# Rotary embedding on one core: two rows of slab 3's cast, instead of three, ahead of the last row of slab 1

## The chip, the cores and the metric

The kernel runs on one core of a Trainium2 chip. The metric is the device time of one launch in microseconds (us). Three runs of the kernel before took 163.22, 163.46 and 164.78 us; their median is 163.46.

## The reference

The input x has 16 batches of 512 positions of 1024 values in float32. The 1024 values are 16 heads of 64, and each head is two halves of 32. Each position has 32 cosines and 32 sines, the same for all heads and batches.

```python
x = x.reshape(batch, seq, num_heads, head_dim)
x1, x2 = x[..., :half_dim], x[..., half_dim:]
rotated = np.concatenate([
    x1 * cos - x2 * sin,
    x1 * sin + x2 * cos
], axis=-1)
return rotated.astype(np.float32)
```

Input and output are 33.55 MB each.

## The kernel before, in words

**Tiles.** The 8192 rows (batch times position) of 1024 values are cut into four pairs of slabs: 0-1, 2-3, 4-5 and 6-7. In a pair each of the 128 partitions holds 16 consecutive rows, 8 of the even slab and 8 of the odd one. A slab is thus 128 partitions x 8192 float32 (32 KB a partition, 4 MB in all). There are three places for a pair in on-chip memory (`places`); pair 6-7 reuses the place of pair 0-1, so its load must wait until that pair has been stored.

**Work on a slab.** All of it is done in place. `cast` (ScalarE) turns the slab's float32 rows into bfloat16 in the lower half of the same bytes. VectorE (lines 171 and 174) multiplies them by the cosine table into the upper half, then by the signed sine table in the lower half, and adds the latter to the former with the two halves of each head exchanged. `copy_out` (ScalarE) turns the upper half back into float32 over the whole slab. All ScalarE work on slabs goes through the helper `copy`, line 155, which keeps the program's order on that engine. `cast` and `copy_out` take a first and a last element, so that a slab's work can be split by rows of `dim` = 1024 elements.

**Tables.** Cosines and sines of 16 positions each lie in partitions 0, 2 ... 62. Eight matmuls with a matrix of ones and minus ones (`pick`) spread them over all partitions, and the result is kept as two bfloat16 tables, one for even and one for odd slabs.

**Transfers.** All are issued by SyncE (SP) through `issue`, line 66, in the program's order, on one queue. Slabs 0 and 1 are loaded one by one, pairs 2-3 and 4-5 in two halves each, first the even partitions (`EVEN`), then the odd ones (`ODD`). All of these are issued in the first 6 us. Then come, in this order: store 0-1 even and odd, load 6-7 even and odd, store 2-3, store 4-5 even and odd, store 6-7. A load of 6-7 waits for the store of the same partitions to land.

**Order around the change.** The loop over `passes` takes slab 0 in two halves, slab 7 in three pieces and every other slab whole. In the pass of a slab the cast of the next slab is issued first, then VectorE's three instructions, then the copy. In the pass of slab 1, ScalarE casts slab 2, copies all rows of slab 1 but the last (`LAST[1]` is one row), casts the first `PART` elements of slab 3, and copies slab 1's last row. Store 0-1 waits for that last row. The rest of slab 3 is cast in the pass of slab 2, from element `PART` on, and VectorE's work on slab 3 waits for that.

Of the kernel before, what the change touches and what calls it, by code (L numbers as in the profile page):

```python
# [2 lines left out]

# [4 lines left out]


@with_exitstack  # L10
def kernel(
    ctx: ExitStack,
    tc: tile.TileContext,
    x: bass.AP,
    cos: bass.AP,
    sin: bass.AP,
    num_heads: int,
    out: bass.AP,
):
    nc = tc.nc  # L20
    P = nc.NUM_PARTITIONS

    batch, seq, dim = x.shape
    nh = num_heads
    hd = dim // nh
    half = hd // 2
    bf16 = mybir.dt.bfloat16
    f32 = mybir.dt.float32

    nb = 2  # L30
    nslabs = batch // nb
    rpp = nb * seq // P
    W = rpp * dim
    TP = seq // (2 * rpp)
    TS = P // TP // 2
    TW = 2 * rpp * half

    out_flat = out.rearrange("b s h d -> b s (h d)")

    singles = ctx.enter_context(tc.tile_pool(name="singles", bufs=1))  # L40
    pairs = ctx.enter_context(tc.tile_pool(name="pairs", bufs=3))
    psum = ctx.enter_context(tc.tile_pool(
        name="psum", bufs=1, space=bass.MemoryType.PSUM))


    def view(t, offset, *dims):
        return dataclasses.replace(t, offset=t.offset + offset,
                                   ap=[t.ap[0], *[list(d) for d in dims]])

    places = [pairs.tile([P, 2 * W], f32, tag="pair", name="pair") for _ in range(3)]


    def here(s, n=1):
        return view(places[s // 2 % 3], s % 2 * W, (1, n * W))


    def there(t, s, n=1):  # L60
        return bass.AP(tensor=t.tensor, offset=t.offset + s // 2 * 2 * P * W + s % 2 * W,
                       ap=[[2 * W, P], [1, n * W]])


    def issue(out, in_):
        tc.keep_in_program_order(nc.sync.dma_start(out=out, in_=in_))  # L66


    def load(s, n=1, parts=slice(None)):
        issue(here(s, n)[parts], there(x, s, n)[parts])  # L70


    def store(s, n=1, parts=slice(None)):
        issue(there(out_flat, s, n)[parts], here(s, n)[parts])


    EVEN, ODD = slice(0, P, 2), slice(1, P, 2)


    load(0)  # L80


    cos_sb = singles.tile([P, TW], f32, tag="cos_sb")
    sin_sb = singles.tile([P, TW], f32, tag="sin_sb")
    for t, src in ((cos_sb, cos), (sin_sb, sin)):
        nc.vector.memset(t, 0.0)  # L86
        issue(t[:TP * TS:TS], bass.AP(
            tensor=src.tensor, offset=src.offset, ap=[[TW, TP], [1, TW]]))

    load(1)  # L90
    for s in (2, 4):
        for parts in (EVEN, ODD):
            load(s, 2, parts)


    pick = singles.tile([P, 2 * P], bf16, tag="pick")
    nc.gpsimd.memset(pick, 0.0)  # L97
    for g in range(2):
        part = view(pick, g * P, (TP, P // TP), (1, TP))
        nc.gpsimd.affine_select(  # L100
            out=part, in_=part, compare_op=mybir.AluOpType.not_equal,
            fill=1.0 - 2.0 * g, base=0, pattern=[[0, P // TP], [-TS, TP]],
            channel_multiplier=1)

    tab1 = singles.tile([P, 2 * TW], bf16, tag="tab1")
    for i, t in enumerate((cos_sb, sin_sb)):
        nc.vector.tensor_copy(out=view(tab1, i * TW, (1, TW)), in_=t)  # L107

    accs, tabs = [], []
    for h in range(2):  # L110
        acc = psum.tile([P, 2 * rpp * hd], f32, tag=f"acc{h}", name="acc")
        for i in range(2):
            for f in range(2):
                nc.tensor.matmul(  # L114
                    view(acc, i * rpp * hd + f * half, (hd, rpp), (1, half)),
                    view(pick, i * f * P, (1, P)),
                    view(tab1, i * TW + h * rpp * half, (half, rpp), (1, half)),
                    start=True, stop=True)
        accs.append(acc)
        tabs.append(singles.tile([P, 2 * rpp * hd], bf16, tag=f"tab{h}", name="tab"))  # L120
    nc.vector.tensor_copy(out=tabs[0], in_=accs[0])  # L121

    PART = 3 * dim
    LAST = {1: dim, 3: dim // 2}
    passes = []
    for s in range(nslabs):
        r = 0  # L130
        for n in {0: (4, 4), nslabs - 1: (4, 2, 2)}.get(s, (rpp,)):
            passes.append((s, r, n))
            r += n


    def halves(u):
        s, r, n = u
        t = here(s).bitcast(bf16)
        return [view(t, (2 * r + i * n) * dim, (1, n * dim)) for i in range(2)]


    def cast(u, a=0, b=None):
        s, r, n = u
        m = (n * dim if b is None else b) - a
        copy(view(halves(u)[0], a, (1, m)), view(here(s), r * dim + a, (1, m)))


    def copy_out(u, a=0, b=None):
        s, r, n = u
        m = (n * dim if b is None else b) - a  # L150
        copy(view(here(s), r * dim + a, (1, m)), view(halves(u)[1], a, (1, m)))


    def copy(out, in_):
        tc.keep_in_program_order(nc.scalar.copy(out=out, in_=in_))  # L155


    for i, u in enumerate(passes):
        s, r, n = u
        if i == 0:  # L160
            cast(u)
            cast(passes[1])
            copy(tabs[1], accs[1])
            cast(passes[2])
        elif s > 0 and not r:
            for v in passes:
                if v[0] == s + 1:
                    cast(v, PART if v[0] == 3 else 0)
        lo, up = halves(u)
        for t, a in ((up, 0), (lo, rpp * hd)):  # L170
            nc.vector.tensor_mul(  # L171
                out=t, in0=lo,
                in1=view(tabs[s % 2], a + r * hd, (hd, n), (0, nh), (1, hd)))
        nc.vector.tensor_add(  # L174
            out=up, in0=up, in1=view(lo, half, (hd, n * nh), (-half, 2), (1, half)))

        if s == 1:
            copy_out(u, 0, n * dim - LAST[s])
            cast((3, 0, rpp), 0, PART)
            copy_out(u, n * dim - LAST[s])  # L180
            for act in (store, load):
                for parts in (EVEN, ODD):
                    act(0 if act is store else 6, 2, parts)
        elif s == 3:
            copy_out(u, 0, n * dim - LAST[s])
        else:
            copy_out(u)
        if s == 4:
            copy_out((3, 0, rpp), rpp * dim - LAST[3])
            store(2, 2)  # L190
        elif s > 4 and s % 2 and r + n == rpp:
            for parts in (EVEN, ODD) if s == 5 else (slice(None),):
                store(s - 1, 2, parts)


# [1 line left out]
_INS = ['x', 'cos', 'sin', 'num_heads']  # L197
_OUTS = [((16, 512, 16, 64), 'float32')]

_NUMBERS = {'num_heads': 16}  # L200


# [26 lines left out]
```

## Time and profile before

| | |
|---|---|
| median of three runs | 163.46 us |
| time of the profiled execution | 163.04 us |
| its span, first to last instruction | 161.2 us |
| busy: DMA engines / ScalarE (ACT) / VectorE (DVE) | 97.5% / 71% / 68% of the span |
| moved | 67.24 MB, 417 GB/s over the span |
| landing of loads 2-3 odd, 4-5 odd | 42.67, 62.02 us |
| issue of store 0-1, even and odd half | 59.46 and 60.03 us |
| landing of store 0-1, even and odd half | 71.68 and 81.56 us |
| landing of load 6-7, odd half | 102.46 us |
| issue of the last store | 139.12 us |

A profile tells of one execution. Times are counted from the start of its span. The share of the DMA engines is the mean over 16 of them. A DMA is issued by an instruction on SP's queue (SPq); some time later its packets run on the engines, and it lands when the last of them has signalled. In a line of the groups, `128x3072 bf16<-128x3072 f32 x1 | 2.7, 2747 | 0.0` means one instruction that writes 3072 bfloat16 elements in each of 128 partitions from as many float32 elements, busy for 2.7 us, 2747 ns each, with no idle time ahead of it. In a table of stretches each row has the stretch, its length, the busy time of each engine with its number of instructions, the granted clock, the share of the DMA engines and their rate.

### The profile page before, as it was taken

The numbers are of one execution on the slowest core, as the hardware profiler recorded it, in microseconds if no ns is written. First come the engines' busy times: TensorE is split into PE (matmuls) and PEld (weight loads), VectorE is DVE, ScalarE is ACT, GpSimd is POOL, SyncE is SP. The second block draws the span as 40 slices with busy tenths as digits, with TensorE's granted clock in tenths as the row PEclk, the third lists the DMA queues.
The fourth block names the chain that finished last, engine by engine and source line by source line (L and its number), as shares of the span: only waits on it lengthen the run. The fifth ranks groups of instructions, "written<-read, shape, count | busy, mean of one in ns | idle before, by whom it ended". The sixth has DMA issues, their size and how long they took to land.

```text
span 161.2 us, 178 instructions
## 1 busy us (share of the span) xinstructions
PE 1.9 (1%) x8; PEld 1.1 (1%) x8; DVE 109.7 (68%) x38; ACT 114.3 (71%) x27; POOL 1.1 (1%) x7
## 2 busy tenths in 40 slices
PE   0004000000000000000000000000000000000000
PEld 0002000000000000000000000000000000000000
DVE  2004999999806998999899999908999998000000
ACT  3007949992399999999999994599999969500000
POOL 2000000000000000000000000000000000000000
DMA  7999999979979979979799899899899899896990
GB/s 260 390 395 418 488 423 520 455 325 520 455 325 520 455 325 520 455 325 520 260 488 455 358 488 455 358 488 455 358 488 455 358 488 455 358 488 293 520 488 33
DMA packets 1472, 67.24 MB, mean 417 GB/s; under 512 B 256, under 2 KB 256, under 8 KB 320
## 3 DMA queue, kind: packets, MB, share of 16 engines
q1 hardware_dynamic: 1472, 67.24, 97.5%
HBM read 33.69 MB, written 33.55 MB: 417 GB/s over the span
## 4 chain that ended last, share of the span: by engine, by line
DMA 50%; DVE 14%; ACT 13%; issue 6%; ACTq 2%; SPq 1%
DMA pair<-in_x_dram 37%; DMA out_dram<-pair 13%; ACT pair L155 13%; DVE pair L171 10%; DVE pair L174 4%; ACTq L224 1%; SPq L66 1%; DVE sin_sb L86 0%; DVE cos_sb L86 0%; ACTq L155 0%
## 5 line engine op out<-in xcount | busy, mean ns | idle before, releaser
L155 ACT CAST pair<-pair 128x8192 bf16<-128x8192 f32 (+11 forms) x25 | 112.2, 4557 | 24.0 <-DMA pair<-in_x_dram 22.6
L171 DVE TENSOR_TENSOR pair<-pair,tab 128x8192 bf16<-128x8192 bf16 (+2 forms) x22 | 71.4, 3258 | 13.1 <-ACT pair L155 12.6
L174 DVE TENSOR_TENSOR pair<-pair 128x8192 bf16<-128x8192 bf16 (+2 forms) x11 | 35.8, 3258 | 0.3
L107 DVE CAST tab<-cos_sb 128x512 bf16<-128x512 f32 x1 | 0.4, 426 | 11.6 <-DMA cos_sb<-in_cos_dram 11.6
L114 PE MATMUL acc<-tab,pick 128*128 128x256 bf16 x8 | 1.9, 415 | 14.0 <-DVE tab L107 14.0
L121 DVE CAST tab<-acc 128x1024 bf16<-128x1024 f32 x1 | 1.2, 1226 | 1.0 <-PE acc L114 1.0
L155 ACT ACT_TABLE_LOAD x1 | 1.3, 1283 | 0.7 <-PEq L210 0.7
L114 PEld LDWEIGHTS <-pick 128*128 128x128 bf16 x8 | 1.1, 140 | 14.3 <-issue 12.4
L86 DVE MEMSET cos_sb<- 128x512 f32 x1 | 0.5, 485 | 0.9 <-PEq L210 0.9
L155 ACT CAST tab<-acc 128x1024 bf16<-128x1024 f32 x1 | 1.0, 1004 | 0.0
L100 POOL TENSOR_SCALAR_AFFINE_SELECT pick<-pick 128x128 bf16<-128x128 bf16 x2 | 0.6, 308 | 0.1
L86 DVE MEMSET sin_sb<- 128x512 f32 x1 | 0.5, 485 | 0.1
L107 DVE CAST tab<-sin_sb 128x512 bf16<-128x512 f32 x1 | 0.4, 427 | 0.0
L97 POOL MEMSET pick<- 128x256 bf16 x1 | 0.3, 311 | 0.3 <-POOLq L210 0.3
L210 POOL MEMSET const-bfloat16-1.0<- 128x1 bf16 x1 | 0.1, 101 | 0.0
L210 POOL MEMSET const-uint8-127<- 128x1 uint8 x1 | 0.1, 101 | 0.0
L210 POOL MEMSET const-float32-0.0<- 128x1 f32 x1 | 0.1, 98 | 0.2 <-issue 0.2
L210 POOL MEMSET const-float32-1.0<- 128x1 f32 x1 | 0.1, 98 | 0.0
## 6 DMA issues: line engine op xcount, KB each, us to landing
pair<-in_x_dram SPq DMA_DIRECT2D x2, 4096.0 KB, 16.5
pair<-in_x_dram SPq DMA_DIRECT2D x6, 34.3
out_dram<-pair SPq DMA_DIRECT2D x6, 21.4
cos_sb<-in_cos_dram SPq DMA_DIRECT2D x1, 64.0 KB, 12.0
sin_sb<-in_sin_dram SPq DMA_DIRECT2D x1, 64.0 KB, 11.8
```

The costliest lines, as they stand in the source:

```text
L66: tc.keep_in_program_order(nc.sync.dma_start(out=out, in_=in_))
L86: nc.vector.memset(t, 0.0)
L97: nc.gpsimd.memset(pick, 0.0)
L100: nc.gpsimd.affine_select(out=part, in_=part, compare_op=mybir.AluOpType.not_equal, fill=1.0 - 2.0 * g, base=0, pattern=[[0, P // TP], [-T ...
L107: nc.vector.tensor_copy(out=view(tab1, i * TW, (1, TW)), in_=t)
L114: nc.tensor.matmul(view(acc, i * rpp * hd + f * half, (hd, rpp), (1, half)), view(pick, i * f * P, (1, P)), view(tab1, i * TW + h * rpp * ...
L121: nc.vector.tensor_copy(out=tabs[0], in_=accs[0])
L155: tc.keep_in_program_order(nc.scalar.copy(out=out, in_=in_))
L171: nc.vector.tensor_mul(out=t, in0=lo, in1=view(tabs[s % 2], a + r * hd, (hd, n), (0, nh), (1, hd)))
L174: nc.vector.tensor_add(out=up, in0=up, in1=view(lo, half, (hd, n * nh), (-half, 2), (1, half)))
L210: nc = _bacc.Bacc("TRN2", target_bir_lowering=False, num_devices=1)
L224: with _tile.TileContext(nc) as tc:
```

## The change

`PART` is the number of elements of slab 3 in each partition that ScalarE casts ahead of slab 1's last row. It goes from three rows to two; the other rows of slab 3, six instead of five, are cast behind it.

```diff
-    PART = 3 * dim
+    PART = 2 * dim
     LAST = {1: dim, 3: dim // 2}
```

The two lines that use it stand unchanged:

```python
cast(v, PART if v[0] == 3 else 0)      # line 168, in the pass of slab 2
cast((3, 0, rpp), 0, PART)             # line 179, in the pass of slab 1
```

## The prediction

> **What bounds the kernel now.** I read the page's first three parts first, then a table of stretches, the chain that ended last, the groups by form and SyncE's timeline.
>
> ```profile
> PE 1.9 (1%) x8; PEld 1.1 (1%) x8; DVE 109.7 (68%) x38; ACT 114.3 (71%) x27; POOL 1.1 (1%) x7
> DMA  7999999979979979979799899899899899896990
> q1 hardware_dynamic: 1472, 67.24, 97.5%
> ```
>
> ScalarE and VectorE are busy about 70% of the span, the 16 DMA engines 97.5%, on one queue. The dips to 7 in the DMA row are no idle time: a packet is counted in the slice in which it starts. In the packet records of the trace every engine moves 64 KB packets of 2.42 us, and 16 of them, one for each engine, make a round. So I cut the stretches at the start of each round:
>
> ```profile
> core 0: us, PE busy (x) PEld busy (x) DVE busy (x) ACT busy (x) POOL busy (x), PEclk, DMA share, GB/s
> 56.10:58.52 2.42, 0.00 (x0) 0.00 (x0) 2.42 (x1) 2.42 (x2) 0.00 (x0) 1.00 1.00 433
> 58.52:60.94 2.42, 0.00 (x0) 0.00 (x0) 2.39 (x2) 2.42 (x2) 0.00 (x0) 1.00 1.00 433
> 60.94:63.37 2.43, 0.00 (x0) 0.00 (x0) 2.21 (x1) 2.43 (x1) 0.00 (x0) 1.00 1.00 432
> 63.37:65.80 2.43, 0.00 (x0) 0.00 (x0) 1.97 (x1) 2.43 (x2) 0.00 (x0) 1.00 1.00 432
> ...
> 77.92:80.74 2.82, 0.00 (x0) 0.00 (x0) 2.82 (x1) 2.82 (x1) 0.00 (x0) 1.00 1.01 372
> 80.74:83.41 2.67, 0.00 (x0) 0.00 (x0) 2.64 (x2) 2.67 (x1) 0.00 (x0) 1.00 1.05 393
> 83.41:85.90 2.49, 0.00 (x0) 0.00 (x0) 2.49 (x1) 2.49 (x2) 0.00 (x0) 1.00 0.98 421
> ```
>
> The rounds that start at 56.11 and 58.53 are the last two of the loads of slabs 4 and 5; the one at 60.95 is the first of store 0-1, the store that the change concerns. The step from load to store is 2.42 us, as within either, share 1.00 and 432 GB/s. Packet by packet, each engine's first store packet begins within 0.03 us of the end of its last load packet: the first engine at 60.95, the last at 61.52. The last three rows are the only slow patch of size, where the store of 0-1 ends and the load of 6-7 begins.
>
> The chain that ended last tells another story:
>
> ```profile
> 3.83 38.84 DMA pair<-in_x_dram
> ...
> 49.68 9.77 ACT pair L155 x3
> 59.45 0.02 issue
> 59.46 0.52 SPq L66
> 59.99 0.04 issue
> 60.03 21.53 DMA out_dram<-pair
> ```
>
> It runs through ScalarE's three instructions (7 rows of copy, 3 rows of cast, 1 row of copy) into the issue of the store, as if each microsecond saved there came off the end. But it follows who released whom, and a DMA's 21.53 us hold its time in the queue. The first packet starts 1.49 us after the first issue at 59.46, at the moment the engine's load packet ends. The table is the judge: the queue, not the issue, sets the start.
>
> **The change part by part.** PART falls from 3072 to 2048 elements. ScalarE's first piece of slab 3 shrinks from 3 rows to 2, the rest grows from 5 rows to 6. Nothing else differs in any engine's order, and no wait is added or removed.
>
> ```profile
> L155 ACT CAST pair<-pair 128x5120 bf16<-128x5120 f32 x1 | 4.5, 4453 | 0.0
> L155 ACT CAST pair<-pair 128x2048 bf16<-128x2048 f32 x2 | 3.7, 1892 | 0.0
> L155 ACT CAST pair<-pair 128x3072 bf16<-128x3072 f32 x1 | 2.7, 2747 | 0.0
> ```
>
> The first piece goes from 2747 to 1892 ns: the copy of slab 1's last row, and the issues of store 0-1 behind it, come 0.855 us earlier: even half at 58.60 instead of 59.46, odd half at 59.17 instead of 60.03.
>
> The 6-row cast has no row. A row costs 853 ns between the rows of 5120 and 3072 ((4453 - 2747) / 2), so I take 4453 + 853 = 5306 ns. The bounds are 4453 (5 rows) and 6160 (the 7-row copy, whose direction differs; at 8 rows the two directions agree, 7017 and 7014). The two pieces then take 1892 + 5306 = 7198 ns where they took 2747 + 4453 = 7200. Slab 3's cast still ends at 63.80, where VectorE, idle for 0.68 us, waits for it. By the bounds it ends 0.85 earlier or 0.86 later. Earlier gains nothing, as below. Later, VectorE idles 5.16 us before slab 6 at 109.59 and absorbs it; ScalarE runs without a gap to the copy behind which store 2-3 is issued at 98.67, and with 0.86 more and the 0.85 from issue to packets (below) that store would come at 100.38, where the first engine is free at 100.41. So I take nothing, and nothing at either end.
>
> What can the 0.855 us buy? The engines are free for the store from 60.95 to 61.52. How long an issue takes to become packets is seen where the queue is empty:
>
> ```profile
> 59.46 0.52 SPq L66 DMA_DIRECT2D out_dram<-pair  x1
> ...
> 139.12 0.35 SPq L66 DMA_DIRECT2D out_dram<-pair  x1
> ```
>
> The last store, issued at 139.12, finds most engines idle, and its first packets on these start from 139.97 to 140.12: 0.85 to 1.00 us. The very first load takes from 0.73 to 1.73 at its quickest engine and 2.45 at its slowest: 1.00 to 1.72. By the nearer row, the store of 0-1 could have started at 59.46 + 0.85 = 60.31 on the first engine, 60.46 on the last: 0.64 us before the earliest is free. By the cold row it would be 60.46 to 61.18, 0.49 us early at the earliest and 0.34 at the latest. It was ready in both, so the gain is 0; lead grows from about 0.6 to 1.5 us and is not spent.
>
> The Trainium skill, "DMA: Bandwidth & Descriptors" (Rules for kernel authors, with the fixed cost under Anatomy of one DMA), says to issue a DMA early so that its fixed cost of about 2 us lies under other work. By that figure the store would be ready at 61.46, half a microsecond late, and the change would gain up to 0.5 us. The trace does not agree: the round at 60.95 is on time with 1.49 us of lead.
>
> What follows is unchanged too. On SP's queue stand, behind the two stores, the even load of 6-7 (waits for the even store to land, 71.68) and the odd one (81.56); both landings come from the DMA engines' rounds, which don't move. Then slab 6's cast at 102.54 follows the odd load's landing, and the last store VectorE and ScalarE behind that cast.
>
> The sum: own time of the profiled execution 163.04 (span 161.25, 1.79 around it) + 0.00 (store) + 0.00 (ScalarE, -2 ns) = 163.04. The runs' median is 163.46, 0.42 above; I carry that over and forecast **163.4**.
>
> **The rivals.**
>
> *Store late without the profiler (faster).* The queue is on time in the one execution that I see, by 0.34 to 0.64 us; another could have the packets come later than the engines. The price is bounded by the whole shift, 0.855 us: 163.46 - 0.86 = 162.6. For it: the runs spread over 1.56 us. Against: store issue and load rounds hang on the same landing at 42.67, so a delay of one moves both. It would be within 1%.
>
> *The slow patch goes away (faster).* The rounds at 77.93 to 83.42 should take 3 x 2.42 and take 2.82 + 2.67 + 2.49: 0.72 us lost at the first engine; the last one, from 76.02 to 90.02 over five rounds of 2.42, lost 1.9. If its place came from when the stores were issued, an earlier issue could remove it: 163.46 less 0.7 to 1.9 gives 161.6 to 162.7, and 160.9 if the round that waits for the last store (3.13 us behind the one before, 0.71 more than 2.42) is on time as well. Against: the issues next to it, of the loads of 6-7, don't move.
>
> *The early store disturbs the loads (slower).* The slow patch stands where a transfer of the other direction had been in the queue for long: the even load, issued at 71.70, nine microseconds ahead. The load-to-store turns at 60.95 and 100.41 (store issued at 98.67), whose stores came in less than 2 us ahead, show none. If store descriptors that wait behind running loads bring it, the change makes a second patch at 60 us, at the same price, 0.7 to 1.9: 164.2 to 165.4, middle 164.8, and up to 167.3 if each half of the store is hit. It decides from the point where descriptors reach an engine before its last load packet has started (58.53 to 59.10). After the change they come at 58.60 + 0.85 = 59.45, 0.35 us past that point, so I hold it unlikely, but the margin is small.
>
> The Trainium skill, the same page (Two DMAs through the same engine are not ordered), says that descriptors of a queue start in order but are pipelined, with reading and writing in separate queues. That would let a waiting store read while loads still write; the records of the turn at 60.95 show no packet longer than 2.44 us.
>
> **How the numbers follow.** About 1% (1.6 us) is what a measurement of this kernel can tell from no change. Hidden: 0.62, own range 162.9 to 164.3, within 1%. Late store: 0.07, within 1%. Patch gone: 0.10, of which 0.06 over 1% faster (below 161.8: with the last store's round, or near the full price), 0.04 within. Disturbed loads: 0.21, of which 0.13 over 1% slower (above 165.1: both halves, or near the full price), 0.08 within. So 0.06 faster, 0.81 same (0.62 + 0.07 + 0.04 + 0.08), 0.13 slower. For 8 in 10 the range runs from between the late store (162.6) and the middle of the patch gone by itself (162.2), 162.3, to past the middle of the disturbed loads, 165.0.
>
> **What would show it.** Right: the 3072 cast is a 2048 cast of about 1.89 us, the 5120 one a 6144 one of about 5.31; first store issued near 58.6 us; the first store round still steps 2.42 us behind the last load round, near 60.95; even store landing near 71.7; slab 3's products starting near 63.8. Wrong: a store round that starts before 60.9 or an on-time landing that moves by more than 0.3 us (a start was hidden in the issue after all); packets over 2.6 us between 58 and 64 us (disturbed loads); rounds at 78 to 85 us back at 2.42 (patch gone); slab 3's products later than 64.3.

## The result and the profile after

The changed kernel takes 161.39 us (median of 18 runs, 161.15 to 162.26), the kernel before 163.3 us (median of 18 runs, 161.69 to 164.78). The ratio is 0.990, 95% interval 0.988 to 0.992: faster by 1.0%. The forecast was no change, 163.4 us, with a range from 162.3. It was wrong. The profiled execution took 161.26 us, its span 159.5, 1.7 less than before.

ScalarE's groups by form between 55 and 62 us (the last two columns of a line are busy time with the mean ns of one, and idle time) show that the change did to the engines what was worked out (5306 and 1892 ns), within 2 ns:

```profile
L155 ACT CAST pair<-pair 128x6144 bf16<-128x6144 f32 x1 | 5.3, 5307 | 0.0
L155 ACT CAST pair<-pair 128x2048 bf16<-128x2048 f32 x1 | 1.9, 1894 | 0.0
```

Slab 3's first product starts at 63.71 (63.83 before). The table of stretches, cut at the rounds of 16 packets again (the columns that matter are the length, second, and the last two, DMA share and GB/s), shows the rest:

```profile
58.70:61.13 2.43, 0.00 (x0) 0.00 (x0) 2.43 (x1) 2.43 (x1) 0.00 (x0) 1.00 1.00 432
61.13:63.55 2.42, 0.00 (x0) 0.00 (x0) 1.90 (x1) 2.42 (x1) 0.00 (x0) 1.00 1.00 433
75.65:78.07 2.42, 0.00 (x0) 0.00 (x0) 1.93 (x2) 2.42 (x2) 0.00 (x0) 1.00 1.00 433
78.07:80.50 2.43, 0.00 (x0) 0.00 (x0) 2.43 (x1) 2.43 (x1) 0.00 (x0) 1.00 1.00 432
80.50:82.96 2.46, 0.00 (x0) 0.00 (x0) 2.43 (x2) 2.46 (x1) 0.00 (x0) 1.00 1.00 426
82.96:85.37 2.41, 0.00 (x0) 0.00 (x0) 2.41 (x1) 2.41 (x2) 0.00 (x0) 1.00 1.00 435
```

The first store round begins at 61.14, no earlier than before (60.95). The turn from load to store was on time before and is on time now. What has gone is the slow patch twenty microseconds later, at the turn from store to load: the last store round and the first two load rounds took 2.82, 2.67 and 2.49 us, and take 2.43, 2.46 and 2.41. The chain that ended last says it in its own way:

```profile
49.56 8.92 ACT pair L155 x3
58.48 0.02 issue
58.49 0.52 SPq L66
59.02 0.04 issue
59.06 22.70 DMA out_dram<-pair
81.76 0.02 issue
81.78 18.93 DMA pair<-in_x_dram
100.71 0.02 issue
```

ScalarE's three instructions are 0.85 us shorter (8.92 for 9.77), and the store gives that back: 22.70 us from issue to landing instead of 21.53, for it waits longer in the queue. The odd store lands at 81.76, 0.20 later than before. But the load behind it takes 18.93 us where it took 20.88, and lands at 100.71 instead of 102.46. These 1.75 us reach the end whole: the last store is issued at 137.38 (139.12 before) and lands at 158.65 (160.41).

### The profile page after: what moved, and what is told of

Its sections match the earlier page's. It is cut to its first block, busy times and chain, and to the rows that moved or that the text cites. A ratio compares the mean times of both kernels' runs of the same rounds, so it can differ in the third digit from the quotient of the medians.

```text
span 159.5 us, 178 instructions
## 1 busy us (share of the span) xinstructions
PE 1.9 (1%) x8; PEld 1.1 (1%) x8; DVE 109.7 (69%) x38; ACT 114.3 (72%) x27; POOL 1.1 (1%) x7
## 4 chain that ended last, share of the span: by engine, by line
DMA 50%; DVE 15%; ACT 12%; issue 6%; ACTq 2%; SPq 1%
DMA pair<-in_x_dram 36%; DMA out_dram<-pair 14%; ACT pair L155 12%; DVE pair L171 10%; DVE pair L174 4%; ACTq L224 2%; SPq L66 1%; DVE sin_sb L86 0%; DVE cos_sb L86 0%; ACTq L155 0%
## 5 line engine op out<-in xcount | busy, mean ns | idle before, releaser
L155 ACT CAST pair<-pair 128x8192 bf16<-128x8192 f32 (+10 forms) x25 | 112.2, 4557 | 22.3 <-DMA pair<-in_x_dram 20.8
```

## The experiments

**The question.** The store was issued about a microsecond earlier, started no earlier, and the turn from the store to the next load became cheap. The packet records of the kernel before hold a hint. Its engines reached the store at different times, 60.95 to 61.52, and thus with different leads over the one issue at 59.46. The engine with the least lead (1.49 us) lost 0.85 us in its last store packet, the one with the most (2.06) lost 0.24; over the 16 engines, lead and that loss go against each other with a correlation of -0.71. (The records do not name the engine: packets are joined where one starts as another ends, and where several fit, the pairing is a best guess.)

**Theory A.** An engine reads ahead of what it writes. How far depends on how long a store's descriptors were there before its last load packet ended; this lead is kept through the store, and it covers the first reads of the next load. **Rivals:** a threshold on the odd half's arrival (B); the sizes of ScalarE's pieces (C); descriptors that wait behind running loads disturb these, from the prediction; later, how the store begins (A2) and the costs of the experiment itself (A3).

**First group: the lead, varied through PART, and the pieces kept with an early issue.**

`part25`, `part35` and `part1` change one number, to 2.5, 3.5 and 1 rows:

```diff
-    PART = 3 * dim
+    PART = 5 * dim // 2        # part25;  7 * dim // 2 in part35,  dim in part1
```

> PART is 2.5 rows, so the store of 0-1 is issued half way, near 59.0 us. Theory A (lead): each engine reads ahead of what it writes, and how far is set by the time between the arrival of the store's descriptors and the end of the engine's last load packet; that lead is kept through the whole store and is what covers the first reads of load 6-7, so the loss at 78 to 85 us shrinks as the lead grows. Lead, issue to first store packet: 1.49 us with 3 rows, 2.65 with 2 rows, here about 2.0: loss between, nearer to none, 161.4 to 162.4 us. Theory B (a threshold on the odd half): the patch comes only when the odd half of the store arrives after the first packet of the even half; here it is issued at about 59.6 and in time, so no patch at all, 161.4. Theory C (sizes of ScalarE's pieces): says nothing firm.

> PART is 3.5 rows, issue near 59.9 us, lead about 1.05 us, the store still on time at 60.95 by the 0.85 us seen from issue to packet. Theory A: the patch at 78 to 85 us is deeper than with 3 rows: first packets there lose 0.6 to 1.3 us instead of 0.2 to 0.9, total 163.7 to 164.8. Theory B: odd half is late as with 3 rows, same patch, 163.3. A plain late store would show at 61 us, not at 78.

> PART is one row, issue near 57.6 us, lead about 3.5 us. Theory A: lead beyond what the engine can use, no patch, 161.4 as with 2 rows. Theory B: same, 161.4. The rival of the prediction, that descriptors waiting behind running loads disturb them: here they arrive at 58.5, before or as the last load packets start (58.5 to 59.1), so packets over 2.6 us between 58 and 64 and more than 161.9.

`copyfirst` keeps 3 rows, but copies slab 1's last row ahead of them:

```diff
             copy_out(u, 0, n * dim - LAST[s])
-            cast((3, 0, rpp), 0, PART)
             copy_out(u, n * dim - LAST[s])
+            cast((3, 0, rpp), 0, PART)
```

> PART stays 3 rows, but slab 1's last row is copied ahead of these 3 rows, so the store is issued near 56.8 us (4.1 us of lead) with ScalarE's pieces as before. Theory A and B: no patch, 161.4. Theory C (the pieces of 3 and 5 rows by themselves bring the loss, whatever the issue): 163.3.

**Second group: the lead of the odd half alone.** `odd_late` starts from the changed kernel (2 rows), with the even half issued early. The odd half and the loads of 6-7 are issued in the pass of slab 2, behind a copy of 32 bytes that has to wait for the first `LATE` elements of slab 2's copy. `odd_mid` differs in `LATE` alone. `small_copy` puts the 32 bytes between the halves with nothing to wait for. `part4` is PART with 4 rows.

```diff
+    LATE = 23 * dim // 4       # odd_late;  9 * dim // 2 in odd_mid
...
         if s == 1:
...
+            store(0, 2, EVEN)
+        elif s == 2:
+            copy_out(u, 0, LATE)
+            issue(scratch, view(here(2), LATE - 8, (1, 8))[0:1])
+            store(0, 2, ODD)
+            for parts in (EVEN, ODD):
+                load(6, 2, parts)
+            copy_out(u, LATE)
```

> PART is 2 rows, so the even half of store 0-1 is issued near 58.5 us with 2.6 us of lead, as in the changed kernel. The odd half's issue is held back, by a copy of 32 bytes that waits for 5.75 rows of slab 2's copy, to near 69.3 us: about 1.5 us ahead of its first packet near 70.8, the lead that the whole store had with 3 rows. Theory A (the read lead is set anew wherever the queue is short of descriptors, and kept from there): the patch at 78 to 85 us is back, first packets there 0.2 to 0.9 us longer, total 162.9 to 163.7, though the first half was early. Rival A2 (what counts is how the store begins: the lead or queueing of the even half at the turn from load to store): no patch, 161.4 to 161.7.

> As odd_late in everything but the split of slab 2's copy, 4.5 rows instead of 5.75, so that the odd half is issued near 68.2 us, about 2.6 us ahead of its first packet. Theory A: no patch, 161.4 to 161.7. Rival A3 (the changed order, the split of slab 2's copy or the small copy costs the time, not the lead): the same as odd_late.

> PART is 2 rows; the copy of 32 bytes stands between the two halves of the store, but waits for nothing that is late, so that both halves are issued near 58.5 to 59.6 us. All theories: no patch, 161.4 to 161.6; more would be the small copy's own cost.

> PART is 4 rows, issue near 60.3 us, lead about 0.65 us if the store could begin on time. By the 0.85 us from issue to packet that the last store showed, it is 0.2 us late at the earliest engine, on time at the last. Theory A: little or no lead is left; the turn at 78 us loses no less than with 3.5 rows (1.05 us in the mean), total 163.4 to 164.6. A theory in which the patch is there or not there (a threshold): 163.3 plus the 0.2 late.

**What was measured.** Times are medians; the ratio is to the kernel before on the same chip, with its 95% interval. The lead is from the start of the issue to the first packet, at the earliest engine; for `odd_late` and `odd_mid` it is that of the odd half. Where the last load packet is stretched (part1, copyfirst), the lead contains the stretch. The next three columns are means over the 16 engines of one execution, from the packet records: the last load packet ahead of the store, the last store packet ahead of the next load (both 2.42 when undisturbed), and the loss at that second turn, which is the time from the start of the last store packet to the start of the engine's fourth packet behind it, less 4 x 2.418 us. The column behind it is when the last engine starts its packet in the fourth round after the turn's first load round.

| kernel | issue | lead | last load packet | last store packet | loss at the turn | last engine | us | ratio |
|---|---|---|---|---|---|---|---|---|
| part4 | 60.70 | 1.18 | 2.42 | 3.13 | 0.81 | 92.04 | 162.84 | 1.001 (0.997 to 1.004) |
| part35 | 60.07 | 1.20 | 2.42 | 3.04 | 0.99 | 92.10 | 163.36 | 1.004 (1.001 to 1.007) |
| before | 59.46 | 1.49 | 2.42 | 2.86 | 0.99 | 92.44 | 163.3 | |
| part25 | 59.06 | 1.98 | 2.42 | 2.52 | 0.15 | 90.74 | 161.42 | 0.991 (0.988 to 0.993) |
| after | 58.49 | 2.65 | 2.42 | 2.44 | 0.04 | 90.59 | 161.39 | 0.990 (0.988 to 0.992) |
| part1 | 57.77 | 3.46 | 2.54 | 2.42 | 0.01 | 90.81 | 161.54 | 0.993 (0.990 to 0.996) |
| copyfirst | 56.92 | 4.71 | 3.00 | 2.42 | -0.01 | 91.34 | 161.85 | 0.992 (0.990 to 0.995) |
| odd_late | 69.75 | 1.21 | 2.42 | 3.11 | 1.07 | 92.32 | 163.26 | 1.000 (0.996 to 1.003) |
| odd_mid | 68.66 | 2.10 | 2.42 | 2.51 | 0.12 | 90.87 | 161.63 | 0.989 (0.982 to 0.995) |

`small_copy` took 161.68 us, ratio 0.990 (0.984 to 0.995).

**What follows.**

*The lead counts, nearly as a step (part25, part35, part4).* The last store packet grows as the lead shrinks: 2.44, 2.52, 2.86, 3.04, 3.13 us. The whole loss at the turn does not grow with it: it is 0.15 us in part25, and 0.8 to 1.0 us in the kernel before, part35 and part4 alike. The last store round of part25, at its first engine (2.82 in the kernel before, 2.43 after the change):

```profile
77.93:80.47 2.54, 0.00 (x0) 0.00 (x0) 2.54 (x1) 2.54 (x1) 0.00 (x0) 1.00 0.99 413
```

Engine by engine, over the nine profiles of the table, the 61 with less than 1.9 us of lead lose 0.98 us in the mean and no less than 0.55; the 75 with more than 2.1 us lose 0.24 us at most; eight lie between and lose from 0.06 to 1.09. Within the kernel before, the whole loss does not follow the lead (correlation -0.08): an engine that loses less in its last store packet loses more behind it. So theory A is right that the lead decides, but its even slope is not what the runs show; a threshold on the lead near 2 us fits the time as well. Theory B's threshold is another one, on the odd half's arrival, and falls with `odd_mid` below: its odd half is issued 7.6 us after the first packet of the even half, and the patch is gone.

Part35's total of 163.36 lies below what theory A forecast (163.7 to 164.8), and the expectation for part4 (163.4 to 164.6) was wrong as well. Part4's store was really late:

```profile
58.87:61.87 3.00, 0.00 (x0) 0.00 (x0) 2.97 (x2) 3.00 (x3) 0.00 (x0) 1.00 0.81 350
61.87:64.30 2.43, 0.00 (x0) 0.00 (x0) 1.75 (x2) 2.43 (x2) 0.00 (x0) 1.00 1.02 432
78.85:81.80 2.95, 0.00 (x0) 0.00 (x0) 2.95 (x1) 2.95 (x1) 0.00 (x0) 1.00 1.06 355
```

In this table of stretches of part4, the engines stand idle for 19% of the first row, and all 16 start the store 1.18 to 1.33 us after its issue. So some 1.2 us is the least that lies between the issue and a packet of this store, and 1.2 us of lead is none. The kernel before had 0.3 us above that at its first engine, part35 nothing, and the turn costs the three about the same. The late start even brings the engines into step: the last of them is at 92.04 in part4 against 92.44 in the kernel before. Both totals also hold a second loss, which the kernel before does not have. Store 2-3 is issued at 98.85 us in part35 and at 99.05 in part4, and the last load packets ahead of it take up to 3.09 and 3.04 us; the last engine is 0.67 and 0.39 us later for it.

*The pieces do not count (copyfirst).* With pieces of 3 and 5 rows as before, the patch is gone: theory C falls. But copyfirst is slower than expected (161.85, not 161.4), and the table of its stretches says where:

```profile
56.31:58.73 2.42, 0.00 (x0) 0.00 (x0) 2.39 (x2) 2.42 (x2) 0.00 (x0) 1.00 1.00 433
58.73:61.62 2.89, 0.00 (x0) 0.00 (x0) 2.89 (x1) 2.86 (x2) 0.00 (x0) 1.00 1.04 363
...
78.53:80.95 2.42, 0.00 (x0) 0.00 (x0) 2.42 (x1) 2.42 (x1) 0.00 (x0) 1.00 1.00 433
80.95:83.36 2.41, 0.00 (x0) 0.00 (x0) 2.38 (x2) 2.41 (x1) 0.00 (x0) 1.00 1.01 435
```

The last load round, ahead of a store that has been in the queue since 56.92, takes 2.89 us at the first engine; the turn to the next load is free. Part1 has a trace of the same: 2.54 us in the mean, packets up to 2.77, where its expectation named packets over 2.6 us and a total over 161.9 for this rival; the total, 161.54, stayed under. So the prediction's rival of the disturbed loads exists. At which lead it begins is not settled. At the turn to store 0-1 it shows with 3.46 us and not with 2.65; ahead of store 2-3 the stretched engines of part35 had 2.4 to 3.6 us from the issue to their first store packet, while the kernel before had up to 3.4 there without any stretch.

*The lead is set wherever the queue runs short, and is kept from there (odd_late, odd_mid).* Here the small copy took 0.79 us of SyncE's time, so that the odd half was issued later than planned, with 1.21 and 2.10 us instead of 1.5 and 2.6. SyncE's timeline and the stretches of odd_late:

```profile
58.70 0.52 SPq L66 DMA_DIRECT2D out_dram<-pair  x1
68.91 0.79 SPq L66 DMA_DIRECT2D scratch<-pair  x1
69.75 0.52 SPq L66 DMA_DIRECT2D out_dram<-pair  x1
```

```profile
61.27:63.69 2.42, 0.00 (x0) 0.00 (x0) 1.96 (x1) 2.42 (x1) 0.00 (x0) 1.00 1.00 433
70.95:73.36 2.41, 0.00 (x0) 0.00 (x0) 2.38 (x2) 2.41 (x2) 0.00 (x0) 1.00 1.01 435
75.80:78.22 2.42, 0.00 (x0) 0.00 (x0) 1.70 (x2) 2.42 (x2) 0.00 (x0) 1.00 1.00 433
78.22:81.35 3.13, 0.00 (x0) 0.00 (x0) 3.13 (x1) 3.13 (x1) 0.00 (x0) 1.00 0.99 335
81.35:83.95 2.60, 0.00 (x0) 0.00 (x0) 2.57 (x2) 2.60 (x1) 0.00 (x0) 1.00 1.03 403
```

The even half starts on time with 2.6 us of lead, the odd half starts on time too, at 70.96, and the patch is back in full, 163.26 us. The same order with the odd half issued 1.09 us earlier has none:

```profile
78.04:80.53 2.49, 0.00 (x0) 0.00 (x0) 2.49 (x1) 2.49 (x1) 0.00 (x0) 1.00 1.01 421
80.53:82.97 2.44, 0.00 (x0) 0.00 (x0) 2.40 (x2) 2.44 (x1) 0.00 (x0) 1.00 1.01 430
```

So neither the beginning of the store (A2) nor the new order or the small copy (A3) makes the patch, and odd_late and odd_mid differ in nothing else but the place of the split, 5.75 and 4.5 rows; small_copy adds about 0.3 us at most (161.68 against 161.39, from different groups of runs). What counts is the lead of the last piece of store ahead of the load.

**What stays open.** That the lead is one of reading over writing is inferred. The records show packets, not an engine's two sides. The Trainium skill, "DMA: Bandwidth & Descriptors" (Two DMAs through the same engine are not ordered), says that descriptors of one queue start in order but are pipelined and that reading and writing have separate queues. That fits: a lead won at one turn can be kept for twenty microseconds by an engine whose sides run at one rate. The profiles agree in one more point. Of the turns that follow a store, only the one to a load is hit: in the profile after, store 2-3 starts with 1.35 to 1.71 us of lead, and its turn to store 4-5 at 119.22 costs nothing. No run separates this from other reasons why a load should suffer, and none says why the load ahead of store 2-3 is stretched in part35 and part4 alone.

No version here beats the changed kernel; part25 equals it. In the profile after, the rounds of the DMA engines follow each other with steps of 2.41 to 2.45 us (means over the engines) from 22.4 us to the end, so no round is left that shows such a loss.

## Why the prediction was wrong, point by point

**What bounds the kernel** was right for the start of the store: the queue of the DMA engines sets it, not the issue that the chain names. The issue counted all the same, one turn further on. The change to ScalarE was right to 2 ns (1894 and 5307 ns measured), and so was the store's start: on time before and after. The issue (58.49), the even landing (71.61), slab 3's first product and the first store round are where they were expected.

**The failed step** is the sentence that lead grows from about 0.6 to 1.5 us and "is not spent", with the term "0.00 (store)". The lead was spent, twenty microseconds later, at the turn to the next load. In the profiled executions the term should have been -1.75 us, by which the odd load of 6-7 lands earlier: 2.82 + 2.67 + 2.49 against 2.43 + 2.46 + 2.41 at the first engine is 0.68, and the last engine, which sets the landing of the load, lost 1.9 before and next to nothing after (its round at 92.44 is now at 90.59).

**The rival that came true** is the slow patch that goes away, with a price of 0.7 to 1.9 us and a chance of 0.10. The price held, at its upper end: the medians differ by 1.91 us. The further price, 160.9 for a last store on time, did not come: that round is on time in the profile after, but the last engine had not waited for it before either, since it went on at 140.75 without a gap. The reason against it ("the issues next to it, of the loads of 6-7, don't move") looked at the wrong neighbours: these issues stand in the queue for nine microseconds anyway, and what decides the turn is how long the store ahead of it had been issued before its packets began.

**The cause named for the patch** was turned round. The prediction saw that the one turn with a patch had its transfer queued long ahead, and feared that an early store would bring a second one. Early queueing does cost something (part1, copyfirst), but the patch in question came from a store queued too late. The reading that the stores of the turns without a patch came in less than 2 us ahead holds for the first engine alone: at the turn at 100.41 the last engine started its store packet at 102.10, 3.43 us after the issue, and its load packet was not stretched.

**Issue to packet** was taken as 0.85 to 1.00 us, from the last store of the kernel before; its packets started on engines that stood idle, but it is one DMA over 128 partitions. The half stores of 64 partitions need 1.18 to 1.33 us (part4). The lead that looked like 0.64 us to spare was 0.3. The 2 us that the prediction took from the Trainium skill, "DMA: Bandwidth & Descriptors" (Anatomy of one DMA), are given there for DMAs that GpSimd issues, and most of them for what follows the last byte; they are no time to the first packet of a store that SyncE issues, and 1.18 to 1.33 us stand in their place.

**Late store without the profiler** fell: the profiled executions show the gain themselves (163.04 to 161.26 us), the first store round in them is on time from 3.5 rows down and late only with 4, and the rival's price, 0.86 us at most, is less than half of the gain. Some runs of the kernel before are nearly as fast as the changed kernel: 7 of the 66 in the three groups of runs took 161.26 to 161.92 us. Its engines had 1.49 to 2.06 us of lead, close to the 2 us at which the loss goes, so a few tenths more may have spared these runs the patch. That is argued and not shown, for none of them was profiled.

## What to carry to other kernels

When the DMA engines never idle, look at each turn of direction in the packet records and not only for gaps: 16 packets longer than their neighbours are lost time too, and their cause may lie one turn of direction earlier. Issue a transfer that follows one of the other direction so that its descriptors arrive ahead of need, but not far ahead: here, for store 0-1, 2.0 to 2.7 us from issue to first packet (at the earliest engine) cost 0.15 us or less per engine, 1.5 and less cost about 1 us at the next turn to a load, 3.5 and more stretched the load ahead. The upper limit may not carry over, for ahead of store 2-3 some loads were stretched with 2.4 us already. A slack that is "hidden anyway" is worth an experiment when a slow stretch of unknown cause stands downstream of it.

## What the runs showed of the hardware that was not expected

- A lead won at the turn from load to store decides the turn from store to load 17 us later (61 and 78 us), through packets that take 2.42 to 2.44 us in the kernel before. An engine with less than 1.9 us of it lost about 1 us there, one with more than 2.1 us 0.24 at most.
- A store of 64 partitions that finds the engines idle has its first packets 1.18 to 1.33 us after its issue; one of 128 partitions needed 0.85 to 1.00 us.
- When store 0-1 was issued 4.7 us ahead of its first packet, the last load packet before it took 3.00 us in the mean instead of 2.42, and the next turn was free.
- Engines that lose time at a turn lose it unequally (0.3 to 2.1 us in the kernel before), and the load lands with the last of them: a mean loss of 1.0 us per engine became 1.75 us in the landing of the load and of the last store.
